# Strassen's form for 14 of 22 gate/up pairs in four feed-forward networks

## The chip, the cores and the metric

One core of a Trainium2 (trn2) chip runs the whole program. The metric is device time in microseconds (us) of one launch, the median of several runs. Engines: PE is TensorE, DVE VectorE, ACT ScalarE, POOL GpSimd; SP issues the loads of weights.

## The reference, cut to what matters

Two blocks follow each other on 512 tokens of width 1024, all in float32. The first has two layers, each with a SwiGLU network, a mixer and another SwiGLU network, and a layer norm after each. The four SwiGLU networks are what the change touches (d_ff 2816):

```python
def swiglu_ffn(x, wi, wo):
    gate, up = jnp.split(x @ wi, 2, axis=-1)
    return (jax.nn.silu(gate) * up) @ wo

def first_block(x, ...):
    alpha = DEEPNORM_ALPHA
    for l in range(DEPTH):
        x = layer_norm(alpha * x + 0.5 * swiglu_ffn(x, ffn1_wi[l], ffn1_wo[l]), ln_g[l, 0], ln_b[l, 0])
        ...
        x = layer_norm(alpha * x + mix, ln_g[l, 1], ln_b[l, 1])
        x = layer_norm(alpha * x + 0.5 * swiglu_ffn(x, ffn2_wi[l], ffn2_wo[l]), ln_g[l, 2], ln_b[l, 2])
    return x
```

The second block (attention branches and a third kind of feed-forward network) is not touched.

## The kernel before, in words

Activations lie transposed: eight tiles of 128 rows (of the width, index k) by 512 tokens. A float32 product is made in three passes of a rounded type: every operand is a high part (the value rounded) and a low part (what is left), and `mm3` (L404) issues weights-high x activations-high, weights-high x activations-low and weights-low x activations-high into one bank of PSUM. The eight tiles of an activation are the objects `X` with lists `h` and `l`.

Weights come in *slabs*, planned ahead in a queue by `plan_w`: a slab is one tile of 128 output columns by 1024 rows, in two raw tiles `wr` of 128x512 (256 KB each). `_dma` (L336) issues the loads on SP up to `raw_bufs` slabs ahead; `_split_hi` (L355) lets ACT copy `wr` into `wh`; `_split_lo` (L364) lets DVE subtract, `wl` = `wr` - `wh`; `slab` (L389) hands out the next slab and splits others ahead, as far as `hl_bufs` allows. The matmuls are thus `m<-xh,wh`, `m<-xl,wh`, `m<-xh,wl`.

One network is `ffn_block1` (L730). It has three parts, `PARTS` (L452): pairs 0 to 5, 6 to 13 and 14 to 21, where pair j is the j-th 128 columns of gate and of up. In each part the pairs are computed (`gemm_tile`, L573, one bank of 512 tokens per slab), then their products go through the down projection (`down`, L678; `out_proj_ln`, L685, in the last part), added to eight tiles `ys`. In part 0 `gemm_first` (L555) does pairs 0 and 1 (four slabs, banks `mf`) as the layer norm's rows come out, and then eight DVE additions make `ys` from the high and low parts. A generator `unit` finishes each pair: silu on ACT (`sg`), product on DVE (`hf`), and the split of it (`hh` on ACT, `hl` on DVE). The last four output tiles run by halves of 256 tokens (banks `mh`), so that the layer norm of the first half begins earlier.

The order of instructions on each engine is written by a scheduler class: `g.s.upto`, `g.s.wait` and `g.s.pump` emit side work (generators that are spawned, here the layer norm's halves) between the matmuls by costs that it holds for each operation. The order stands fixed in the program. All DVE, ACT, POOL and SP instructions are recorded by one helper (L55), all matmuls by another (L279), so rows are told apart by tiles.

Of the kernel before, what the change touches and what calls it, by code (L numbers as in the profile page):

```python
# [223 lines left out]


class G:


    def __init__(self, ctx, tc, raw_bufs=3, hl_bufs=8, f_bufs=90, q_bufs=16):
# [101 lines left out]
    def plan_w(self, w, c0, cols, k0, kt):  # L331

        src = w[k0 * P:(k0 + kt) * P, c0:c0 + cols].rearrange("(k p) c -> p k c", p=P)
        self.plan(lambda t, k, n: self.nc.sync.dma_start(t, src[:, k:k + n]), kt, cols)

    def _dma(self):  # L336
        while self.wi_dma < len(self.wq) and self.wi_dma < self.wi_split + self.raw_bufs:
            load, kt, cols = self.wq[self.wi_dma]
            per = NT // cols
            self.whl_t[self.wi_dma] = parts = []  # L340
            for k0 in range(0, kt, per):
                n = min(per, kt - k0)
                t = self.f("wr", F32, n * cols)
                load(t.rearrange("p (k c) -> p k c", c=cols), k0, n)
                parts.append(t)
            self.wi_dma += 1

    def split_ahead(self, n=1):

        self._dma()  # L350
        while n > 0 and self.wi_split < min(len(self.wq), self.wi_done + self.hl_bufs):
            self._split()
            n -= 1

    def _split_hi(self):  # L355
        parts = []
        for t in self.whl_t[self.wi_hi]:
            hi = self.f("wh", F32R, t.shape[1])
            self.nc.scalar.activation(hi, t, AF.Copy)
            parts.append((t, hi))  # L360
        self.whl_t[self.wi_hi] = parts
        self.wi_hi += 1

    def _split_lo(self):  # L364
        j = self.wi_split
        cols = self.wq[j][2]
        hl = []
        for raw, hi in self.whl_t[j]:
            lo = self.f("wl", F32R, raw.shape[1])
            self.nc.vector.tensor_tensor(lo, raw, hi, ALU.subtract)  # L370
            for k in range(lo.shape[1] // cols):
                c = slice(k * cols, (k + 1) * cols)
                hl.append((hi[:, c], lo[:, c]))
        self.whl_t[j] = hl
        self.wi_split += 1
        self._dma()

    def _split(self):

        if self.wi_hi == self.wi_split:  # L380
            self._split_hi()
        if self.wi_hi == self.wi_split + 1 and self.wi_hi < min(len(self.wq), self.wi_done + self.hl_bufs):
# [68 lines left out]
ALPHA = 4.0 ** 0.25  # L451
PARTS = ((0, 6), (6, 8), (14, 8))  # L452


# [263 lines left out]

def plan_ffn(g, w_a, w_b, hook=None):
    for k0, n in PARTS:  # L720
        for j in range(k0, k0 + n):
            g.plan_w(w_a, j * P, P, 0, KD)
            g.plan_w(w_a, 2816 + j * P, P, 0, KD)
# [6 lines left out]
def ffn_block1(g, xs, gv, bv, hook=None, into=None, by_half=True):  # L730

# [4 lines left out]
    for pi, (k0, n) in enumerate(PARTS):  # L736
        hs = {}

        def unit(j, pg, pu):
# [10 lines left out]
            hs[j] = (hh, hl)  # L750

        j = k0
        if pi == 0:
# [5 lines left out]
            for k in range(KD):  # L759
                nc.vector.tensor_tensor(ys[k], xs.h[k], xs.l[k], ALU.add)  # L760
        while j < k0 + n:
            ps = [gemm_tile(g, xs)]
            pipe.add(unit(j, lambda: ps[0], lambda: ps[1]))
            ps.append(gemm_tile(g, xs))
            pipe.step()
            j += 1
# [1885 lines left out]
def kernel(ctx: ExitStack, tc: tile.TileContext, d, out: bass.AP):  # L2652
# [25 lines left out]
    plan_ffn(g, d["ffn1_wi"][0], d["ffn1_wo"][0])  # L2678
    plan_even(g, d["ev_w_in"][0], d["ev_w_out"][0])
    plan_ffn(g, d["ffn2_wi"][0], d["ffn2_wo"][0])  # L2680
    plan_ffn(g, d["ffn1_wi"][1], d["ffn1_wo"][1])
    plan_odd(g, d["od_w_in"][0], d["od_w_out"][0], lambda l: plan_mem(g, d["w_mem_kv_2"][l]))
    plan_ffn(g, d["ffn2_wi"][1], d["ffn2_wo"][1])
    for l in range(2):
# [25 lines left out]
    with man("f3"):  # L2710
        rx = ffn_block1(g, x, *ln(1, 2),
                            into=lambda: RX(g, [g.f("x") for _ in range(KD)], v["g_pre_mix0"]))
    for l in range(2):
# [41 lines left out]
```

## Time and profile before

| what | value |
|---|---|
| median of 3 runs | 3696.52 us (3695.84 to 3699.57) |
| the profiled execution's own time | 3691.82 us |
| its span (first to last instruction) | 3689.6 us |
| mean granted clock of PE | 0.989 of full speed |
| PE busy | 98% |
| DVE busy | 56% |
| ACT busy | 40% |
| POOL busy | 10% |
| read from memory over the span | 323.65 MB |

The page is one profiled execution. Busy shares are means over the span. The chain is followed back from the last instruction, at each step to what released it. In a timeline a row is one instruction (or a few alike in a row, with their number): its start, its duration, engine, line, operation, tile written and tiles read; in brackets the idle time before it and who ended that. A row's duration on DVE includes a tail in which the next one already runs, so the distance of starts is shorter. In the first part of a network PE runs `mf`, then the `m` of pairs 2 to 5, then `mg` and `m` of the down projection.

### The profile page before, as it was taken

Reading aid. Unit: us, or ns where it says so; the run is one execution under the profiler, and the core shown is the slowest. Engines: PE = TensorE matmul, PEld = TensorE weight load, DVE = VectorE, ACT = ScalarE, POOL = GpSimd, SP = SyncE. Lnnn points to the kernel's source line nnn. Section 1 sums busy time; section 2 is a strip of 40 time slices with the busy share of each in tenths; the row PEclk is TensorE's granted clock in tenths of the full one; section 3 lists DMA queues with packets and bytes.
Section 4 is the critical chain, followed back from the end, with each engine's and each line's share of the span. In section 5 each row is a group of like instructions: output and inputs, shape, how many; then the busy total and the mean of one; then the engine's idle time right before and its main releaser. Section 6 shows DMA issues by size and latency. Waiting matters only on the chain.

```text
span 3689.6 us, 52324 instructions
## 1 busy us (share of the span) xinstructions
PE 3633.5 (98%) x19704; PEld 2982.4 (81%) x19704; DVE 2062.8 (56%) x3771; ACT 1460.8 (40%) x2837; POOL 359.2 (10%) x547
## 2 busy tenths in 40 slices
PE   9999999999999999999999999999999999999999
PEld 7888878888888887677888888788888887888888
DVE  4333878432643266767633375557666745467755
ACT  4223664232333236534422353435333444354433
POOL 0001103000200021010100130022000300130001
PEclk9999999999999999989999999999999999999999
DMA  5333222332333221113233333332333332323231
GB/s 158 100 100 84 75 70 87 104 98 86 89 106 97 86 75 52 39 39 98 84 104 98 90 91 118 89 104 67 99 97 90 105 112 85 100 83 101 86 97 52
DMA packets 615087, 331.78 MB, mean 90 GB/s; under 512 B 25234, under 2 KB 608051, under 8 KB 614835
## 3 DMA queue, kind: packets, MB, share of 16 engines
q1 hardware_dynamic: 612018, 324.81, 30.3%
q10 hardware_dynamic: 2816, 3.64, 0.3%
q8 instruction: 154, 2.52, 0.3%
q14 instruction: 99, 0.80, 0.1%
HBM read 323.65 MB, written 4.74 MB: 89 GB/s over the span
## 4 chain that ended last, share of the span: by engine, by line
PE 91%; DVE 6%; ACT 1%; issue 1%; POOL 0%; DMA 0%; SPq 0%; DVEq 0%; POOLq 0%; ACTq 0%
PE m L279 64%; PE mg L279 5%; PE mf L279 4%; PE mh L279 4%; PE tk L279 3%; PE br L279 2%; DVE wl L55 1%; DVE ln_z L55 1%; DVE x L55 1%; DVE rm_t L55 1%; DVE rst L55 1%; PE st L279 1%; DVE xgl L55 0%; PE S L279 0%; PE mv L279 0%
## 5 line engine op out<-in xcount | busy, mean ns | idle before, releaser
L55 DVE TENSOR_TENSOR wl<-wr,wh 128x512 fp32r<-128x512 f32 (+2 forms) x1208 | 815.3, 720 | 114.9 <-ACT wh L55 114.4
L55 ACT ACTIVATE wh<-wr 128x512 fp32r<-128x512 f32 (+2 forms) x1208 | 663.9, 607 | 93.1 <-PE m L279 50.8
L279 PE MATMUL m<-xh,wh 128*128 128x512 f32 x1544 | 619.6, 401 | 0.0
L279 PE MATMUL m<-xh,wl 128*128 128x512 f32 x1544 | 610.9, 396 | 0.0
L279 PE MATMUL m<-xl,wh 128*128 128x512 f32 x1544 | 610.4, 395 | 0.0
L279 PE MATMUL m<-xgh,wh 128*128 128x512 f32 x1184 | 470.7, 398 | 0.0
L279 PE MATMUL m<-xgl,wh 128*128 128x512 f32 x1184 | 466.3, 394 | 0.0
L279 PE MATMUL m<-xgh,wl 128*128 128x512 f32 x1184 | 466.0, 394 | 0.0
L55 DVE SCALAR_TENSOR_TENSOR hf<-sg,m 128x512 f32<-128x512 f32 x80 | 55.0, 688 | 575.0 <-PE m L279 565.7
L279 PEld LDWEIGHTS m<-xh,wh 128*128 128x128 f32 x1544 | 291.0, 188 | 74.6 <-issue 7.3
L279 PEld LDWEIGHTS m<-xh,wl 128*128 128x128 f32 x1544 | 291.0, 188 | 69.1 <-issue 0.4
L279 PEld LDWEIGHTS m<-xl,wh 128*128 128x128 f32 x1544 | 291.2, 189 | 67.6 <-issue 1.7
L279 PEld LDWEIGHTS m<-xgh,wh 128*128 128x128 f32 x1184 | 222.3, 188 | 55.9 <-issue 5.3
L279 PEld LDWEIGHTS m<-xgh,wl 128*128 128x128 f32 x1184 | 222.3, 188 | 52.4
L279 PEld LDWEIGHTS m<-xgl,wh 128*128 128x128 f32 x1184 | 222.4, 188 | 49.9
L279 PE MATMUL m<-hh,wh 128*128 128x512 f32 x600 | 236.5, 394 | 0.0
L279 PE MATMUL m<-hl,wh 128*128 128x512 f32 x600 | 236.3, 394 | 0.0
L279 PE MATMUL m<-hh,wl 128*128 128x512 f32 x600 | 236.2, 394 | 0.0
L55 ACT ACTIVATE sg<-m 128x512 f32<-128x512 f32 x80 | 47.8, 598 | 424.1 <-PE m L279 424.1
L55 ACT ACTIVATE hh<-hf 128x512 fp32r<-128x512 f32 x88 | 55.7, 633 | 382.6 <-DVE hf L55 382.6
L55 ACT ACTIVATE uc<-up,vecs 128x512 f32<-128x512 f32 x88 | 71.7, 817 | 202.3 <-DVE up L55 202.3
L55 DVE SCALAR_TENSOR_TENSOR uc<-up,vecs,uc 128x512 f32<-128x512 f32 x176 | 131.3, 748 | 12.9 <-ACT uc L55 6.8
(546 smaller groups left out, 6330.3 us busy)
## 6 DMA issues: line engine op xcount, KB each, us to landing
wr<-in_ffn_wi_dram SPq DMA_DIRECT2D x352, 256.0 KB
wr<-in_w_up_dram SPq DMA_DIRECT2D x176, 256.0 KB
wr<-in_ffn_wo_dram SPq DMA_DIRECT2D x160, 256.0 KB
wr<-in_w_in_dram SPq DMA_DIRECT2D x152, 256.0 KB
wr<-in_w_down_dram SPq DMA_DIRECT2D x80, 256.0 KB
wr<-in_od_w_in_dram SPq DMA_DIRECT2D x50, 256.0 KB
wr<-in_ev_w_in_dram SPq DMA_DIRECT2D x48, 256.0 KB
wr<-in_w_out_dram SPq DMA_DIRECT2D x32, 256.0 KB
```

Source lines behind the costliest of these rows:

```text
L55: r = fn(*a, **kw)
L279: return self.nc.tensor.matmul(out, lhsT, rhs, start=start, stop=stop, **kw)
```

## The change

14 of the 22 pairs of each network (`FAST`) are computed in Strassen's form (Winograd's variant). The weights of gate and up of one pair, for the upper and lower 512 rows, are the four blocks A11, A12 (gate) and A21, A22 (up); the activations by halves of the width and of the tokens are the four blocks of B. Seven products of 128x512 by 512x256 take the place of eight:

- `Pair` loads the four blocks as raw tiles and forms four sums of weights on DVE (S1 = A21 + A22, S2 = S1 - A11, S3 = A11 - A21, S4 = A12 - S2).
- `Combos` forms four sums of activations for each of four k, once per network, from `ys` before alpha and the down projection are added, on DVE, and splits them (`th` on ACT, `tl` on DVE).
- `Fast` runs the products in the order A11, S2, A12, S3, S1, A22, S4, each 4 x 3 matmuls of 256 tokens, into four banks, and adds up the banks by `c1` and `c2` on ACT and DVE. `unit_fast` then ends the pair as `unit` does.
- The low part of S2 and of S1 isn't a DVE subtraction: ACT writes the negated high part and POOL issues a DMA that adds the sum to it.
- The slabs of such a pair are single tiles, seven per pair. While `raw_lim` is set, loads are limited to 6 raw tiles and splits to 7 tiles of high parts, and two slabs at most are split per call. This holds from the sums of activations to the last pair; outside it the limits are as before.

```diff
+class Pair:
+    ORDER = ("A11", "S2", "A12", "S3", "S1", "A22", "S4")
+    BY_DMA = ("S2", "S1")
+    FETCH = {"A11": ("A11", "A21"), "S2": ("A22",), "A12": ("A12",)}
...
+    def factor(self, nm):
+        t, TT = self.t, self.g.nc.vector.tensor_tensor
+        if nm == "A11":
+            return t["A11"]
+        if nm == "S2":
+            t["S1"], t["S2"] = self.g.f("ws"), self.g.f("ws")
+            TT(t["S1"], t["A21"], t["A22"], ALU.add)
+            TT(t["S2"], t["S1"], t["A11"], ALU.subtract)
+            return t["S2"]
+        if nm == "S3":
+            TT(t["A21"], t.pop("A11"), t["A21"], ALU.subtract)
+            return t.pop("A21")
+        if nm == "S4":
+            TT(t["A12"], t["A12"], t.pop("S2"), ALU.subtract)
+            return t.pop("A12")
+        return t[nm] if nm == "A12" else t.pop(nm)
...
     def _dma(self):
-        while self.wi_dma < len(self.wq) and self.wi_dma < self.wi_split + self.raw_bufs:
+        while self.wi_dma < len(self.wq) and (
+                self.raw_tiles(self.wi_split, self.wi_dma) < self.raw_lim if self.raw_lim else
+                self.wi_dma < self.wi_split + self.raw_bufs):
...
+    def room(self, i):
+        if i >= len(self.wq):
+            return False
+        if not self.raw_lim:
+            return i < self.wi_done + self.hl_bufs
+        return sum(1 if isinstance(load, Pair) else -(-kt * cols // NT)
+                   for load, kt, cols in self.wq[self.wi_done:i + 1]) <= self.hl_lim
...
-            self.nc.vector.tensor_tensor(lo, raw, hi, ALU.subtract)
+            if isinstance(self.wq[j][0], Pair) and self.wq[j][1] in Pair.BY_DMA:
+                self.nc.scalar.activation(lo, raw, AF.Copy, scale=-1.0)
+                self.nc.gpsimd.dma_start(lo, raw, accum_op=ALU.add)
+            else:
+                self.nc.vector.tensor_tensor(lo, raw, hi, ALU.subtract)
...
+FAST = (4, 5, 6, 7, 9, 10, 12, 13, 14, 15, 17, 18, 20, 21)
+RAW1, HL1 = 6, 7
...
+class Combos:
...
+        for k in range(4):
+            lo, hi = self.ys[k], self.ys[4 + k]
+            s, u = g.f("ta"), g.f("tb")
+            TT(s[:, a], lo[:, b], lo[:, a], ALU.subtract)
+            TT(s[:, b], hi[:, b], s[:, a], ALU.subtract)
+            yield g.pace()
+            TT(u[:, a], hi[:, b], lo[:, b], ALU.subtract)
+            TT(u[:, b], hi[:, a], s[:, b], ALU.subtract)
+            yield g.pace()
+            for nm, t in (("s", s), ("u", u)):
+                h, l = g.f("th", F32R), g.f("tl", F32R)
+                g.split_x(h, l, t)
+                self.t[nm, k] = (h, l)
...
+class Fast:
+    PLACE = {"A11": ("a", 0), "S2": ("a", 1), "A12": ("b", 0), "S3": ("b", 1), "S1": ("d", 1), "A22": ("d", 0),
+             "S4": ("e", 0)}
...
+        w = g.slab()
+        for k in range(4):
+            x = self.cb(nm, k)
+            g.s.upto(*w[k], *x)
+            g.mm3(self.ps[bank][:, HALF[c]], w[k], x, k == 0, k == 3)
...
+        if nm == "S2":
+            c = self.c1 = g.f("c1")
+            nc.scalar.copy(c[:, a], ps("a")[:, a])
+            TT(c[:, b], c[:, a], ps("a")[:, b], ALU.add)
+        elif nm == "S3":
+            u = self.c2 = g.f("c2")
+            c = self.c1
+            TT(u[:, b], c[:, b], ps("b")[:, b], ALU.add)
+            TT(c[:, a], c[:, a], ps("b")[:, a], ALU.add)
...
+        elif nm == "A22":
+            u, c = self.c2, self.c1
+            TT(c[:, b], c[:, b], ps("d")[:, b], ALU.add)
...
+            TT(v(w), v(ps("d")), u[:, None, b].to_broadcast([P, 2, 256]), ALU.add)
...
+        elif nm == "S4":
+            c = self.c1
+            TT(c[:, b], c[:, b], ps("e")[:, a], ALU.add)
...
+            g.raw_lim, g.hl_lim, g.ahead = RAW1, HL1, 2
+            cb = Combos(g, xs, ys)
+            if fast:
+                g.s.spawn(cb.make())
...
+            g.s.wait(lambda: cb.n == 4)
+            if j not in open_:
+                open_[j] = Fast(g, cb)
+            e = open_[j]
+            e.step(nm)
...
+        if pi == len(PARTS) - 1:
+            g.raw_lim, g.ahead = 0, 1
```

How the rows move on two engines, at three places. In the names, a first number is a buffer's or tile's and the rest tells it from others of the program.

**First place: DVE at the start of the third network, from pair 2 to the first fast pair.** Before, `hf` of pair 2 (`hf_1881`) is followed by lo subtractions, two per slab:

```order
L55 SCALAR_TENSOR_TENSOR hf_1881_8865<-sg_1880_8864,m_1888_8879 128x512
L55 TENSOR_TENSOR wl_1891_8908<-wr_1861_8795,wh_1886_8875 128x512
L55 TENSOR_TENSOR wl_1892_8910<-wr_1862_8797,wh_1887_8877 128x512
L55 TENSOR_TENSOR hl_1890_8906<-hf_1881_8865,hh_1889_8905 128x512
L55 TENSOR_TENSOR wl_1900_8949<-wr_1875_8830,wh_1895_8916 128x512
L55 TENSOR_TENSOR wl_1901_8951<-wr_1876_8832,wh_1896_8918 128x512
L55 SCALAR_TENSOR_TENSOR hf_1899_8947<-sg_1898_8946,m_1906_8961 128x512
```

Now, from `hf` of pair 3 (`hf_2253`) on, the sums of activations for k = 2 (at the dots stand six rows of the same pattern for k = 3, and two lo subtractions), and S1 and S2 of the second fast pair (`ws_2290`, `ws_2291`):

```order
L55 TENSOR_TENSOR tl_2264_10951<-tb_2260_10920,th_2263_10950 128x512
L55 SCALAR_TENSOR_TENSOR hf_2253_10906<-sg_2252_10905,m_2258_10918 128x512
L55 TENSOR_TENSOR ta_2267_10961<-y_2164_10439 128x256
L55 TENSOR_TENSOR tb_2268_10962<-y_2168_10443,y_2164_10439 128x256
L55 TENSOR_TENSOR ta_2267_10961<-y_2168_10443,ta_2267_10961 128x256
L55 TENSOR_TENSOR tb_2268_10962<-y_2168_10443,ta_2267_10961 128x256
L55 TENSOR_TENSOR tl_2270_10968<-ta_2267_10961,th_2269_10967 128x512
L55 TENSOR_TENSOR tl_2272_10972<-tb_2268_10962,th_2271_10971 128x512
...
L55 TENSOR_TENSOR wl_2285_11013<-wr_2225_10778,wh_2284_11011 128x512
L55 TENSOR_TENSOR ws_2290_11035<-wr_2226_10780,wr_2234_10819 128x512
L55 TENSOR_TENSOR c1_2288_11031<-c1_2288_11031,m_2279_10989 128x256
L55 TENSOR_TENSOR ws_2291_11036<-ws_2290_11035,wr_2225_10778 128x512
```

The second half of the sums of activations, three lo subtractions and S1 and S2 of pair 5 now stand behind `hf` of pair 3, which reads a bank that PE must end first.

**Second place: PE in the same network, where the first pair that becomes fast begins (before) and in the second fast pair (now).** Before, each matmul is 512 tokens wide, and its low weights come from DVE:

```order
L279 MATMUL m_1915_9002<-xh_1773_8301,wh_1871_8822 128x512
L279 MATMUL m_1915_9002<-xl_1781_8309,wh_1871_8822 128x512
L279 MATMUL m_1915_9002<-xh_1773_8301,wl_1873_8826 128x512
L279 MATMUL m_1915_9002<-xh_1774_8302,wh_1871_8822 128x512
```

Now (bank `m_2308` has the products of A11 and S2, `m_2312` that of A12; `wl_2293` is the low part of S2 that a DMA writes):

```order
L319 MATMUL m_2308_11137<-xh_2128_10256,wl_2285_11013 128x256
L319 MATMUL m_2308_11137<-th_2248_10872,wh_2292_11039 128x256
L319 MATMUL m_2308_11137<-tl_2249_10873,wh_2292_11039 128x256
L319 MATMUL m_2312_11170<-xh_2129_10257,wh_2296_11060 128x256
L319 MATMUL m_2312_11170<-xl_2137_10265,wh_2296_11060 128x256
L319 MATMUL m_2312_11170<-xh_2129_10257,wl_2297_11062 128x256
...
L319 MATMUL m_2312_11170<-xh_2132_10260,wl_2297_11062 128x256
L319 MATMUL m_2308_11137<-th_2248_10872,wl_2293_11041 128x256
```

Twelve matmuls of A12's product stand between the second matmul of S2 and the first that needs its low part. In the other fast pairs that one comes right behind the second.

**Third place: DVE in the layer norm ahead of the third network, at the end of its first half** (`ln_z` and `xl` are the norm's rows). Before:

```order
L55 SCALAR_TENSOR_TENSOR ln_z_1824_8511<-ln_z_1824_8511,vecs_101,rs1_1795_8342 128x256
L55 SCALAR_TENSOR_TENSOR xl_1787_8315<-ln_z_1808_8466,vecs_101,xh_1779_8307 128x256
L55 SCALAR_TENSOR_TENSOR xl_1788_8316<-ln_z_1824_8511,vecs_101,xh_1780_8308 128x256
L55 SCALAR_TENSOR_TENSOR st_v_1826_8544<-st_1825_8541,st_m2_1827_8545 128x256
L55 TENSOR_TENSOR wl_1839_8672<-wr_1750_8151,wh_1837_8668 128x512
```

Now:

```order
L55 TENSOR_TENSOR wl_2172_10447<-wr_2100_10099,wh_2114_10127 128x512
L55 TENSOR_TENSOR wl_2173_10449<-wr_2101_10101,wh_2115_10129 128x512
L55 SCALAR_TENSOR_TENSOR ln_z_2182_10475<-ln_z_2182_10475,vecs_101,rs1_2147_10294 128x256
L55 SCALAR_TENSOR_TENSOR st_v_2184_10484<-st_2183_10481,st_m2_2185_10485 128x256
L55 SCALAR_TENSOR_TENSOR xl_2139_10267<-ln_z_2160_10418,vecs_101,xh_2131_10259 128x256
L55 SCALAR_TENSOR_TENSOR xl_2140_10268<-ln_z_2182_10475,vecs_101,xh_2132_10260 128x256
```

Two lo subtractions of the fourth slab of the coming network, which were made earlier before, stand ahead of the last two `xl`.

## Rows read from the trace of the kernel before

**Rows 1.** The page: busy time by engine, and the chain's shares by engine.

```profile
PE 3633.5 (98%) x19704; PEld 2982.4 (81%) x19704; DVE 2062.8 (56%) x3771; ACT 1460.8 (40%) x2837; POOL 359.2 (10%) x547
...
PE 91%; DVE 6%; ACT 1%; issue 1%; POOL 0%; DMA 0%; SPq 0%; DVEq 0%; POOLq 0%; ACTq 0%
```

**Rows 2.** The chain in order of time, third network: start, us, engine, tile.

```profile
996.40 18.50 PE mf L279 x156
1014.90 44.50 PE m L279 x192
...
1192.97 122.40 PE m L279 x528
```

**Rows 3.** Window of gate/up: length, busy PE, PEld, DVE, ACT, POOL, clock, DMA share, GB/s.

```profile
811.00:944.00 133.00, 133.00 (x575) 107.71 (x574) 44.81 (x72) 35.36 (x64) 0.00 (x0) 1.00 0.33 95
```

**Rows 4.** Timeline of PE: matmuls of 512 columns, and the last output tiles' of 256.

```profile
899.79 0.39 PE L279 MATMUL m<-xh,wl 128*128 128x512 f32 x1
900.02 0.39 PE L279 MATMUL m<-xh,wh 128*128 128x512 f32 x1
...
362.60 0.28 PE L279 MATMUL mh<-hh,wh 128*128 128x256 f32 x1
...
372.52 0.28 PE L279 MATMUL mh<-hh,wh 128*128 128x256 f32 x1
```

**Rows 5.** Timeline of DVE, in a gate/up stretch and in a layer norm.

```profile
900.29 0.69 DVE L55 SCALAR_TENSOR_TENSOR hf<-sg,m 128x512 f32<-128x512 f32 x1 [7.44 <-PE m L279]
900.90 1.29 DVE L55 TENSOR_TENSOR wl<-wr,wh 128x512 fp32r<-128x512 f32 x2
902.10 0.68 DVE L55 TENSOR_TENSOR hl<-hf,hh 128x512 fp32r<-128x512 f32 x1
...
1000.36 0.74 DVE L55 TENSOR_TENSOR ln_z<-y,st 128x256 f32<-128x256 f32 x2
1001.02 0.88 DVE L55 SCALAR_TENSOR_TENSOR ln_z<-ln_z,vecs,rs 128x256 f32<-128x256 f32 x2
```

**Rows 6.** Timeline of ACT in a gate/up stretch.

```profile
894.71 0.60 ACT L55 ACTIVATE sg<-m 128x512 f32<-128x512 f32 x1 [3.16 <-PE m L279]
895.21 1.14 ACT L55 ACTIVATE wh<-wr 128x512 fp32r<-128x512 f32 x2
```

**Rows 7.** Groups by form: count, busy us, mean ns of one, idle before.

```profile
L55 DVE TENSOR_TENSOR wl<-wr,wh 128x512 fp32r<-128x512 f32 x1118 | 776.2, 737 | 114.4 <-ACT wh L55 113.9
...
L55 DVE TENSOR_TENSOR y<-y,mh 128x256 f32<-128x256 f32 x48 | 19.9, 415 | 21.0 <-PE mh L279 21.0
...
L55 ACT COPY y<-mh 128x256 f32<-128x256 f32 x16 | 5.8, 363 | 11.4 <-PE mh L279 11.4
```

**Rows 8.** Timeline of DVE at the start of the third network.

```profile
1011.15 1.29 DVE L55 TENSOR_TENSOR wl<-wr,wh 128x512 fp32r<-128x512 f32 x2
1015.85 0.69 DVE L55 SCALAR_TENSOR_TENSOR hf<-sg,mf 128x512 f32<-128x512 f32 x1 [3.40 <-ACT sg L55]
1017.23 0.69 DVE L55 TENSOR_TENSOR hl<-hf,hh 128x512 fp32r<-128x512 f32 x1 [0.70 <-ACT hh L55]
1017.84 0.68 DVE L55 SCALAR_TENSOR_TENSOR hf<-sg,mf 128x512 f32<-128x512 f32 x1
1018.44 4.90 DVE L55 TENSOR_TENSOR y<-xh,xl 128x512 f32<-128x512 f32 x8
```

**Rows 9.** The chain: loads that it waited for, at the start and alone.

```profile
7.78 5.66 DMA xs<-in_x_dram
...
562.96 2.62 DMA wr<-in_ffn_wi_dram
```

**Rows 10.** Timelines of DVE and POOL at the end of the first network.

```profile
352.24 2.39 DVE L55 TENSOR_TENSOR wl<-wr,wh 128x512 fp32r<-128x512 f32 x2
...
352.46 1.62 POOL L55 TENSOR_TENSOR sum<-y,y 128x512 f32<-128x512 f32 x1 [250.88 <-ACT sq L55]
```

More of the change, by code (lines that the diff above doesn't have):

```diff
@@ L346, in _dma @@
             self.wi_dma += 1
+    def room(self, i):
[5 more added lines that the diff above has]
+                   for load, kt, cols in self.wq[self.wi_done:i + 1]) <= self.hl_lim
     def split_ahead(self, n=1):
         self._dma()
-        while n > 0 and self.wi_split < min(len(self.wq), self.wi_done + self.hl_bufs):
+        while n > 0 and self.room(self.wi_split):
             self._split()
@@ L356, in _split_hi @@
         parts = []
+        load, nm, _ = self.wq[self.wi_hi]
+        if isinstance(load, Pair):
+            self.whl_t[self.wi_hi] = [load.factor(nm)]
         for t in self.whl_t[self.wi_hi]:
@@ L381, in _split @@
             self._split_hi()
-        if self.wi_hi == self.wi_split + 1 and self.wi_hi < min(len(self.wq), self.wi_done + self.hl_bufs):
+        if self.wi_hi == self.wi_split + 1 and self.room(self.wi_hi):
             self._split_lo()
@@ L716, in out_proj_ln, with pair_order, plan_ffn @@
         g.s.spawn(finish(hf))
-def plan_ffn(g, w_a, w_b, hook=None):
-    for k0, n in PARTS:
-        for j in range(k0, k0 + n):
-            g.plan_w(w_a, j * P, P, 0, KD)
-            g.plan_w(w_a, 2816 + j * P, P, 0, KD)
+def pair_order(js, fast):
+    for j in js:
+        for nm in Pair.ORDER if j in fast else (None,):
+            yield j, nm
+def plan_ffn(g, w_a, w_b, hook=None, fast=()):
+    for k0, n in PARTS:
+        pairs = {}
+        for j, nm in pair_order(range(k0, k0 + n), fast):
+            if nm is None:
+                g.plan_w(w_a, j * P, P, 0, KD)
+                g.plan_w(w_a, 2816 + j * P, P, 0, KD)
+            else:
+                if j not in pairs:
+                    pairs[j] = Pair(g, w_a, j * P, 2816 + j * P)
+                g.plan(pairs[j], nm, P)
         for m in range(KD):
@@ L732, in ffn_block1 @@
+def ffn_block1(g, xs, gv, bv, hook=None, into=None, by_half=True, fast=()):
     nc = g.nc
@@ L750, in unit, with unit_fast @@
             hs[j] = (hh, hl)
+        def unit_fast(j, e):
+            sg, hf = e.c1, e.c2
+            nc.scalar.activation(sg, sg, AF.Silu)
+            yield True
+            nc.vector.scalar_tensor_tensor(hf, sg, 0.5, hf, ALU.mult, ALU.mult)
+            hh, hl = g.f("hh", F32R), g.f("hl", F32R)
+            nc.scalar.activation(hh, hf, AF.Copy)
+            yield True
+            nc.vector.tensor_tensor(hl, hf, hh, ALU.subtract)
+            hs[j] = (hh, hl)
         j = k0
@@ L760, in ffn_block1 @@
                 nc.vector.tensor_tensor(ys[k], xs.h[k], xs.l[k], ALU.add)
[L761 to L766, printed above, removed]
+            g.raw_lim, g.hl_lim, g.ahead = RAW1, HL1, 2
+            cb = Combos(g, xs, ys)
+            if fast:
+                g.s.spawn(cb.make())
+        open_ = {}
+        for j, nm in pair_order(range(j, k0 + n), fast):
+            if nm is None:
+                ps = [gemm_tile(g, xs)]
+                pipe.add(unit(j, lambda: ps[0], lambda: ps[1]))
+                ps.append(gemm_tile(g, xs))
+                pipe.step()
+                continue
+            g.s.wait(lambda: cb.n == 4)
[3 more added lines that the diff above has]
+            e.step(nm)
+            if nm == "S4":
+                pipe.add(unit_fast(j, e))
+                del open_[j]
         pipe.drain()
+        if pi == len(PARTS) - 1:
+            g.raw_lim, g.ahead = 0, 1
         of = lambda k, c=slice(0, NT): (hs[k0 + k][0][:, c], hs[k0 + k][1][:, c])
@@ L2711 @@
         rx = ffn_block1(g, x, *ln(1, 2),
-                            into=lambda: RX(g, [g.f("x") for _ in range(KD)], v["g_pre_mix0"]))
+                            into=lambda: RX(g, [g.f("x") for _ in range(KD)], v["g_pre_mix0"]), fast=FAST)
     for l in range(2):
```

81 lines of the change are left out of this document (73 added, 8 removed).

## The prediction

> **What bounds the kernel now.** I read the shares by engine first, then the chain that ended last, then a window inside a feed-forward network (FFN), then single instructions. TensorE (PE) is busy 98% of the span and carries 91% of the chain [rows 1]. The chain in order of time says the same of the FFN that the change touches: matmul group follows matmul group for 100 us and more with nothing between [rows 2]. In the gate/up stretch from 811 to 944 us PE is busy all of it at granted clock 1.00, so at its upper level of 2.4 GHz, while DVE is busy 45 of 133 us, ACT 35, POOL none, and a third of the DMA capacity is in use [rows 3]. So within these FFNs a microsecond of PE removed is a microsecond of time, as long as the other queues, which have room, keep delivering in time.
>
> **Columns removed.** A plain pair (gate and up) is 2 x 8 x 3 = 48 matmuls of 512 columns. A chain row gives 122.40 us for 528 such [rows 2], 0.2318 each, 11.13 us per pair; the timeline shows one starting every 0.23 [rows 4]. A fast pair is 7 products x 4 x 3 = 84 matmuls of 256 columns (the PE rows of the second place above). Matmuls of that width run before in the last output tiles: from 362.60 to 372.52 stand 84 intervals, 9.92 us, 0.118 each [rows 4], with weights changing as in a fast pair. The gain is 11.13 - 9.92 = 1.21 us per pair; 14 pairs in 4 FFNs are 56, so **-67.8 us**. Granted clock stays: PE was never idle before these rows and, if nothing is late, isn't after.
>
> **What DVE gets.** A queued DVE operation costs what it holds the queue: 1.20 for two of 512 columns (900.90 to 902.10), 0.60 each; 0.66 for two of 256 (1000.36 to 1001.02), 0.33 each [rows 5]. A plain pair costs four lo subtractions, hf and hl, 6 x 0.60 = 3.6 of 11.1 us. A fast pair costs five lo, four sums of weights, one 512-column eviction, hf and hl, 12 x 0.60 = 7.2, and five evictions of 256, 1.65: 8.9 us of 9.92. It fits, narrowly. By the means of single operations (737 and 415 ns for lo and eviction [rows 7], 0.69 for hf) it is 12 x 0.73 + 5 x 0.415 = 10.8, over 9.92 for a run of fast pairs, though two fast and one plain (25.2) still stay under PE's 31.0. I take the queued price, since these operations stand back to back; the other is a rival. ACT gets seven hi copies, two negated ones, an eviction, silu and hh: 11 x 0.57 (1.14 for two [rows 6]) + 0.36 [rows 7] = 6.6 us, hidden. Weights read from memory are the same four tiles of 256 KB.
>
> **The new wait: lo of S2 and S1.** POOL queues 112 accumulating DMAs, two per fast pair; PE needs what they write. No such DMA, and none issued by POOL, is in the trace of before. Call L the time from the end of ACT's negated copy to the landing. Nearest rows are loads that the chain waited for: 2.62 us for one of 256 KB, 5.66 where the first eight came together [rows 9]. An accumulating transfer reads the target too, so below 2.62 isn't plausible; a gain is excluded because PE can't use a tile that isn't there. I take the middle, **L = 4.1**, because a third of the DMA capacity is taken beside it [rows 3], and keep both ends.
>
> Second fast pair of a run (seven places per FFN, 28): when the last matmul of S2 of the pair before ends (t), ACT copies its bank (an engine starts 0.27 after the next matmul began: 899.79, 900.02, 900.29 [rows 4, 5]), DVE adds (0.36 and 0.42 [rows 7]), forms S2 of this pair (0.69), ACT writes hi and the negated copy (1.14 [rows 6]); with hand-offs of 0.1 that is t + 3.2. PE needs the lo after six products and two matmuls, 74 x 0.118 = 8.7. So L up to 5.5 costs nothing: **0 us** at 4.1, 28 x 0.16 = 4.5 at 5.66.
>
> Start of each FFN (four): here DVE has sums of activations to make too, and the second fast pair (j = 5) is the tight one. Count from T0, the end of the first matmul group (1014.90 in the third FFN [rows 2]). DVE comes from hf, hl, hf to the y additions at T0 + 3.5 (1018.44) and needs 4.8 for eight [rows 8]. hf of pair 2 starts at T0 + 11.4, hf of pair 3 waits for PE until T0 + 22.25 + 0.27 = 22.5, and the order (first place above) puts it *ahead* of the sums for k = 2 and 3. From there the rows up to S2 of pair 5 are seven lo or tl, S1's sum and hf at 0.60 and nine of 256 columns at 0.33, 8.4 us, and two waits for ACT's copy of a sum (about 0.55 each: a copy of 0.57 and two hand-offs, less one sum beside it; the wait for hh, 0.70, is its like [rows 8]): S2 starts at 32.0, ends at 32.7, ACT's two copies end at 34.0. PE reaches the matmul that needs its lo after the two plain pairs and 110 narrow matmuls (84, and 26 before it in the order of the second place), 22.25 + 13.0 = 35.2. It is late by L - 1.2: 2.9 us at 4.1, 1.4 at 2.62, 4.5 at 5.66. Four starts: **+11.6 us** (5.7 to 18).
>
> **Lookahead at the borders.** Four layer norms now have two more lo subtractions in front of the last xl of the first half (third place): 2 x 0.60 = 1.2 us, if PE waits there for it. 0 to 1.2 each; I take a quarter, since the norm's rows on DVE wait for PE and ACT as well: **+1 us** (0 to 4.8).
>
> **Sum.** -67.8 + 0 + 11.6 + 1 = -55.2. The profiled execution took 3691.8 (span 3689.6 and 2.2 around), so 3636.6; the median of the runs is 4.7 above that execution, so **3641.3 us**. Own range: -67.8 + 5.7 = -62.1, 3634.4, to -67.8 + 4.5 + 18 + 4.8 = -40.5, 3656.0.
>
> **The rivals.**
> 1. *Nothing is late* (L under 1.5, or PE never reaches the wait). Only for: 2.62 is an upper end if part of it is the issue. -67.8: 3628.7. Chance 0.07.
> 2. *POOL and DVE hold each other up.* For: two lo subtractions took 2.39 us instead of 1.29 when a POOL addition began beside them [rows 10, 8], 1.10 more, and DVE will hardly pause in fast stretches. If POOL gets to issue only when the DVE run in progress ends (1.29 to 2.39, taken as 2.0), L = 6.1: 28 x 0.6 + 4 x 4.9 + 1 = 37.4, -30.4: 3666.1. Against: POOL issues here, and does no arithmetic in these stretches [rows 3]. Chance 0.14. The Trainium skill, "SBUF — State Buffer", section "SBUF: two separate sides", has a rule of this kind: GpSimd can't write the descriptors of its own DMAs while VectorE holds the port pair they share, so that a 620 ns DMA took about 3100. An estimate by that page (4.1 + 2.5) is L = 6.6, 28 x 1.1 + 4 x 5.4 + 1 = 53, so 3682; the row of 2.39 agrees with a shared port, but no run here shows a DMA issued by POOL.
> 3. *DVE becomes the bound.* At 10.8 us per fast pair and the 1.10 twice, for its two accumulating DMAs, 13.0: each second pair is 3.1 behind, less the 1.4 of room at L = 4.1: 28 x 1.7 = 47.6, and 4 x (2.9 + 3.1) + 1 = 25: +4.8, no change, 3701. Against: queued operations took 0.60 in every row read. Without the 1.10: 10.8 is 0.9 over, within the room; 4 x 3.8 + 1 = 16, 3645. Chance of the first 0.03.
> 4. *Slower: the accumulating DMA is slow.* Its place is the same 28 + 4, break-even 28 (L - 5.5) + 4 (L - 1.2) + 1 = 67.8, L = 7.05. If reading the target and writing the sum cost a load each in series, 2.62 + 5.66 = 8.28: 28 x 2.78 + 4 x 7.08 + 1 = 107, +39: 3736. For: two rows' worth of latency is possible for a kind of transfer that no row shows. Against: every 256 KB load ran under 5.7 here. Chance 0.06.
>
> That the change doesn't do what it says is no rival: the order has 84 matmuls of 256 columns in each of 56 pairs. The forecast keeps 0.70.
>
> **How the numbers follow.** Two in a thousand of 3700, about 7 us, is what the measurement tells from no change. The range goes from rival 1 (3628) through the forecast to rival 2 (3668): 0.70 + 0.07 + 0.14 = 0.91, less the tails of the forecast. Faster: 0.70 + 0.07 + 0.14 = 0.91; same 0.03; slower 0.06.
>
> **What would show it.** Right: narrow matmuls 0.118 apart for 9.9 us per fast pair; DVE at about nine tenths there; no PE gap in the second pairs of later runs; four gaps of 1.5 to 4.5 us behind the first fast pair of each FFN, at the first matmul with S2's lo, waiting for a POOL DMA; landings about 4 us after the negated copy. Wrong: gaps at many of the 28 places (rivals 2 and 4 by the landing, 3 by DVE with no pause and on-time landings), or narrow matmuls over 0.13 apart, which would take the first term away.

## The result, and the profile after

The median went from 3698.05 to 3645.6 us (four runs each), -52.5 us; the ratio is 0.9856 with an interval of 0.9835 to 0.9877. The prediction said 3641.3 and a range of 3628 to 3668. The profiled execution of the changed kernel took 3646.0 us, with a span of 3644.3. A second round of runs gave 3650.0 against 3695.1, ratio 0.9869 (0.9848 to 0.989).

The page of the changed kernel, the lines that answer to [rows 1], then the new queue and the new transfers (count, size, median us from issue to landing):

```profile
PE 3575.0 (98%) x21720; PEld 3035.3 (83%) x21720; DVE 2414.9 (66%) x4483; ACT 1651.4 (45%) x3206; POOL 452.9 (12%) x659
...
q0 software_dynamic: 16128, 29.37, 5.0%
...
PE 86%; DVE 8%; ACT 2%; issue 2%; DMA 1%; POOL 1%; SPq 0%; DVEq 0%; ACTq 0%; POOLq 0%
...
wl<-ws POOLq DMA_DIRECT2D x112, 256.0 KB, 3.8
```

PE is busy 58 us less, DVE 352 us more, and a new item is on the chain: DMA, with the transfers that make lo of S2 and S1. The chain in order of time through the third network (to be read against [rows 2]) shows where:

```profile
973.63 18.72 PE mf L319 x157
992.35 32.40 PE m L319 x180
...
1026.15 3.90 DMA wl<-ws
1030.09 7.10 PE m L319 x58
1037.19 8.34 PE mg L319 x36
1045.53 106.89 PE m L319 x708
1152.42 11.14 PE mg L319 x48
1163.56 115.18 PE m L319 x744
```

Behind 1037 the network is one run of matmuls again: 708 and 744 without a wait. Ahead of that, one transfer stands on the chain. The window of the second part's gate/up, six fast and two plain pairs (columns as in [rows 3]):

```profile
1070.50:1152.30 81.80, 81.80 (x602) 77.56 (x601) 57.80 (x106) 41.36 (x78) 8.51 (x10) 1.00 0.54 130
```

PE is busy for all 81.8 us; the same eight pairs took 89.0 before. DVE is at 71%, ACT at half.

**One stretch must be taken out of every comparison.** I cut each profile where the chain shows it: each network from the first matmul behind `mf` to the first `mh`, and what lies between. All but one of these stretches agree between two profiles of one kernel to a microsecond. One doesn't: the odd mixer (third network's half tiles to the fourth's `m`) took 455 to 475 us in thirteen profiles, whatever the kernel. Two profiles of the changed kernel, each cut at the same distances from the start of that stretch (columns as in [rows 3], first the change's first profile, then its second):

```profile
1300.86:1473.00 172.14, 171.03 (x1108) 135.29 (x1107) 135.72 (x315) 104.54 (x220) 24.51 (x36) 1.00 0.18 50
1473.00:1533.00 60.00, 57.81 (x863) 40.23 (x862) 41.40 (x86) 30.41 (x47) 0.30 (x3) 0.91 0.16 42
```

```profile
1301.53:1473.67 172.14, 171.03 (x1108) 135.30 (x1107) 135.72 (x315) 104.53 (x220) 24.50 (x36) 1.00 0.18 50
1473.67:1533.67 60.00, 57.80 (x729) 39.80 (x726) 35.10 (x76) 24.17 (x39) 0.30 (x3) 0.76 0.14 37
```

The first 172 us are alike to the instruction. In the next 60 PE is busy 57.8 us in both, but gets through 863 matmuls at a mean granted clock of 0.91 and through 729 at 0.76 (means over its two levels, 1.2 and 2.4 GHz). So the same program in the same order differs by 14.7 us in this one stretch. A spread of 20 us is also what the runs of the kernel before show (3690 to 3710 us), so medians of single rounds are a poor measure here, and the experiments are read by stretches:

| kernel | median us | ratio to before (95%) | networks 1 to 4, sum | first parts, networks 1 to 4 | even mixer | odd mixer |
|---|---|---|---|---|---|---|
| before | 3698.1 | | 1291.9 | 45.5, 44.3, 44.5, 44.6 | 281.6 | 457.3 |
| before, again | 3695.8 | 0.9988 (0.9972 to 1.0003) | 1291.9 | 45.5, 44.3, 44.5, 44.6 | 281.8 | 463.5 |
| change | 3645.6 | 0.9856 (0.9835 to 0.9877) | 1235.6 | 45.2, 44.4, 44.8, 44.9 | 286.4 | 460.6 |
| change, again | 3650.0 | 0.9869 (0.9848 to 0.989) | 1236.5 | 45.2, 44.6, 44.7, 44.8 | 287.2 | 475.3 |
| limits only | 3703.1 | 1.001 (0.9992 to 1.0029) | 1291.4 | 45.4, 44.2, 44.3, 44.5 | 288.2 | 472.8 |
| lo by DVE | 3643.9 | 0.9843 (0.9818 to 0.9867) | 1228.1 | 43.4, 42.1, 42.4, 44.9 | 286.5 | 455.6 |
| pairs 4, 5 plain | 3650.4 | 0.9859 (0.9837 to 0.988) | 1237.4 | 45.5, 44.3, 44.6, 44.5 | 286.5 | 463.7 |
| borders mended | 3642.0 | 0.9833 (0.9807 to 0.9859) | 1235.9 | 45.3, 44.6, 44.5, 44.9 | 281.4 | 455.4 |
| sums early | 3657.5 | 0.9868 (0.9847 to 0.9889) | 1232.1 | 47.3, 42.6, 43.1, 42.7 | 287.1 | 472.4 |
| all three | 3643.1 | 0.9833 (0.9812 to 0.9855) | 1227.4 | 45.6, 41.9, 42.2, 42.1 | 281.7 | 474.4 |
| 18 pairs | 3626.6 | 0.979 (0.9759 to 0.9822) | 1217.6 | 47.2, 42.3, 43.4, 43.2 | 281.5 | 455.4 |
| 18, lo by DVE | 3612.5 | 0.977 (0.9753 to 0.9787) | 1205.7 | 43.4, 41.9, 42.2, 42.1 | 282.0 | 462.6 |
| 18, S1 by DMA | 3613.9 | 0.9778 (0.9752 to 0.9803) | 1209.9 | 45.1, 43.6, 42.6, 42.2 | 279.9 | 457.7 |

"Even mixer" is the stretch from the first network's half tiles to the second's first `m` behind `mf`, layer norms included; a first part ends with the first `mg`.

### The profile page after: what moved, and what is told of

Its sections match the earlier page's. It is cut to its first block, busy times and chain, and to the rows that moved or that the text cites. A ratio compares the mean times of both kernels' runs of the same rounds, so it can differ in the third digit from the quotient of the medians.

```text
span 3644.3 us, 58033 instructions
## 1 busy us (share of the span) xinstructions
PE 3575.0 (98%) x21720; PEld 3035.3 (83%) x21720; DVE 2414.9 (66%) x4483; ACT 1651.4 (45%) x3206; POOL 452.9 (12%) x659
## 4 chain that ended last, share of the span: by engine, by line
PE 86%; DVE 8%; ACT 2%; issue 2%; DMA 1%; POOL 1%; SPq 0%; DVEq 0%; ACTq 0%; POOLq 0%
PE m L319 61%; PE mg L319 5%; PE mf L319 3%; PE tk L319 3%; PE mh L319 3%; PE br L319 2%; DVE wl L55 1%; DVE ln_z L55 1%; DVE rm_t L55 1%; DVE x L55 1%; DMA wl<-ws 1%; DVE xgl L55 1%; DVE rst L55 1%; PE st L319 0%; DVE y L55 0%
## 5 line engine op out<-in xcount | busy, mean ns | idle before, releaser
L55 DVE TENSOR_TENSOR wl<-wr,wh 128x512 fp32r<-128x512 f32 (+2 forms) x1264 | 858.0, 717 | 236.8 <-ACT wh L55 214.9
L319 PE MATMUL m<-xh,wh 128*128 128x512 f32 (+1 forms) x1320 | 456.0, 345 | 0.1
L319 PE MATMUL m<-xh,wl 128*128 128x512 f32 (+1 forms) x1320 | 447.5, 339 | 0.7 <-DVE wl L55 0.7
L319 PE MATMUL m<-xl,wh 128*128 128x512 f32 (+1 forms) x1320 | 446.2, 338 | 0.0
L319 PEld LDWEIGHTS m<-xh,wl 128*128 128x128 f32 x1320 | 249.7, 189 | 30.8 <-DVE wl L55 1.3
L319 PE MATMUL m<-th,wl 128*128 128x256 f32 x896 | 252.2, 282 | 5.8 <-DMA wl<-ws 5.6
L319 PE MATMUL m<-tl,wh 128*128 128x256 f32 x896 | 251.1, 281 | 0.0
L319 PE MATMUL m<-th,wh 128*128 128x256 f32 x896 | 250.0, 281 | 0.0
L55 POOL DMA_DIRECT2D wl<-ws x112 | 96.2, 859 | 1110.1 <-ACT wl L55 782.1
L319 PEld LDWEIGHTS m<-th,wl 128*128 128x128 f32 x896 | 168.7, 188 | 7.7 <-DMA wl<-ws 7.5
```

The costliest lines, as they stand in the source:

```text
L55: r = fn(*a, **kw)
L319: return self.nc.tensor.matmul(out, lhsT, rhs, start=start, stop=stop, **kw)
```

## The experiments

**Is what lies outside the networks scatter?** The kernel before, unchanged.

> The kernel before, unchanged, profiled a second time. Inside the four networks the profiles agree with 56.4 us of gain, outside them the changed one is 11.1 us longer (of which 4.8 in the even mixer, 3.3 in the odd one). If that is scatter between executions, the stretches outside the networks come out 5 to 11 us longer here than in the first profile, and the ratio to before is 1.000. If the change itself costs it, by the lookahead at the borders, they agree with the first profile within 2 us. Either way each network, from the end of its first matmul group to its first half tile, takes 322.6 to 323.8 us.

Measured: the networks again 1291.9 us in sum, the even mixer 281.8, the odd one 463.5 (6.2 more). So 3.3 us in the odd mixer are within its scatter, and the 4.8 of the even mixer are not: that stretch repeats to 0.2 us. Each side was right on one mixer.

**The limits alone.**

```diff
-FAST = (4, 5, 6, 7, 9, 10, 12, 13, 14, 15, 17, 18, 20, 21)
+FAST = ()
```

> The limits of the weight stream as changed, but no pair in Strassen's form. Theory: the limits cost nothing inside the networks (322.6 to 323.8 us each) and at most 1 us at each of the four borders, so within 4 us of before. Rival: the limits are what makes the rest of the program 11 us longer; then this kernel is 8 to 11 us slower than before, with its loss in the even and odd mixers.

Measured: networks 1291.4, so the limits cost nothing inside. The even mixer took 288.2, 6.5 us more than before, and the stretch between the second and third network 49.2 instead of 47.9. My "at most 1 us at each border" fell here: the limits alone lengthen the even mixer. Without the odd mixer (472.8, within its scatter) the span is 9.2 us longer than before, 6.5 of them in the even mixer, so of the rival the size held, and its place for the larger part.

**lo of S2 and S1 by DVE.**

```diff
-    BY_DMA = ("S2", "S1")
+    BY_DMA = ()
```

> The lo parts of S2 and S1 by DVE subtractions instead of accumulating DMAs. Theory: without the 4.1 us to a landing the wait at the start of each network shrinks from 2.3 to 2.8 us to 0.2 to 1, so 6 to 9 us faster than the change; DVE has 8.9 + 1.2 = 10.1 us per fast pair, 0.2 over PE's 9.9, which the plain pair between runs gives back. Rival: DVE, not the DMA, sets the steady pairs; then the second pairs of the 28 runs come late by 0.3 to 2 us each and the kernel is 5 us or more slower than the change.

Measured: networks 7.5 us shorter than the change; the second and third parts keep 81.7 to 82.0. First parts fall to 42.1 and 42.4 us in networks 2 and 3, where the columns alone ask for 96 x 0.2318 + 168 x 0.118 = 42.1. The chain of the third network has no transfer any more:

```profile
987.36 42.40 PE m L319 x264
1029.76 6.02 PE mg L319 x26
```

The fourth network stays at 44.9, with another wait. Its chain, in order of time:

```profile
1778.61 0.64 ACT th L55
1779.25 0.04 issue
1779.30 0.50 PE m L319 x2
```

PE waits there for the split of the last sum of activations, in the first fast pair: the sums for k = 2 and 3 still stand behind hf of pair 3, and here the split of those for k = 1 too, which in the change stands ahead of it. DVE in the fourth network of this run:

```profile
1771.37 0.69 DVE L55 SCALAR_TENSOR_TENSOR hf<-sg,m 128x512 f32<-128x512 f32 x1 [1.61 <-PE m L319]
1773.28 0.69 DVE L55 TENSOR_TENSOR tl<-ta,th 128x512 fp32r<-128x512 f32 x1 [1.22 <-ACT th L55]
```

The DMA was thus one cause of two, and it bought nothing.

**Pairs 4 and 5 plain.**

```diff
-FAST = (4, 5, 6, 7, 9, 10, 12, 13, 14, 15, 17, 18, 20, 21)
+FAST = (6, 7, 9, 10, 12, 13, 14, 15, 17, 18, 20, 21)
```

> Pairs 4 and 5 plain again, so 12 fast pairs per network, and the sums of activations have until pair 6. Theory: the two pairs at the start gain 4 x 2.42 = 9.7 us in columns and the wait for the sums costs 4 x 2.3 to 2.8 = 10, so dropping them changes nothing: within 2 us of the change, first part 44.5 us, second and third parts as they are. Rival: the columns pay in full and the loss lies elsewhere; then it is 8 to 10 us slower than the change.

Measured: networks 1.8 us longer than the change in sum, with two late landings in the second and third parts of networks 3 and 4 (1.0 and 1.1 us). The two pairs at each start gain in columns what the wait takes back, as the theory had it.

**The borders.** In the last part `ahead` stays 2 until the last down projection is through.

```diff
         if pi == len(PARTS) - 1:
-            g.raw_lim, g.ahead = 0, 1
+            g.raw_lim = 0
...
             out_proj_ln(g, ys, of, n, 4, evac, st, finish, head(g, of, n, 2))
+            g.ahead = 1
```

> The change, but two slabs may still be split per call through the last down projection of each network, so that the fourth slab of the next stage is split before the layer norm and not in it; the order of PE outside the networks is then that of the kernel before. Theory: the 4.7 us that the even mixer takes longer after the change come from that order, in which a chunk of the mLSTM (num, den, S) stands ahead of weight matmuls that used to cover its wait. Then the stretch from the first network's half tiles to the second's first matmul group falls from 286.4 to 281.6 to 282.0, the stretch between the second and third from 48.5 to 47.9, the networks stay at 308.2 to 309.4, and the kernel is 4 to 7 us faster than the change. Rival: the mixer is longer because of what the network leaves behind (its loads or its accumulating DMAs); then it stays at 286.

Measured: even mixer 281.4, second to third network 47.8 (change 48.5), tail behind the fourth network 1572.5 (change 1573.6, before 1572.0), networks as they were. The theory holds for the two stretches that it names; the difference behind the fourth network is no larger than what two profiles of the kernel before differ by (1572.0 and 1572.9). In the even mixer PE's order is again that of before. The chain shows what the other order does; first the kernel before, then the change, then this run, at the same place of the even mixer:

```profile
494.98 9.49 PE m L279 x41
504.47 0.86 PE num L279 x2
```

```profile
485.92 1.28 ACT L55
...
487.22 0.59 ACT E L55
...
489.08 0.61 DVE E L55
...
489.73 2.00 PE num L319 x2
491.73 1.68 PE den L319 x2
```

```profile
481.82 8.34 PE m L319 x36
490.16 0.86 PE num L319 x2
```

Before, 41 weight matmuls run while ACT and DVE prepare E (1.28 us of it a table load, then the exponential), and `num` follows at once. After the change `num` stands ahead of them, and PE waits for E. The wait, from the list of PE's waits in the change, and the windows behind it in the change and, later in the mixer, in the kernel before (columns as in [rows 3]):

```profile
PE num L319 <- DVE E L55: 4.0, 1, 4.0
```

```profile
489.70:493.30 3.60, 3.57 (x5) 1.50 (x6) 2.00 (x4) 3.20 (x6) 0.46 (x1) 0.53 0.00 0
```

```profile
573.40:576.90 3.50, 3.17 (x8) 2.54 (x9) 2.07 (x5) 2.22 (x3) 1.06 (x3) 0.52 0.01 2
```

Behind the 4.0 us without a matmul the granted clock is 0.53, close to the lower level of 1.2 GHz, and `num` and `den` take 3.7 us instead of 1.7. The kernel before has such a stretch too, 84 us later (0.52), in which six `mg` and two `num` take 3.6 us; there the change needs 2.1. So 4.0 us of waiting and 2.0 at the lower clock, less 1.5 that the kernel before loses at the lower clock and the change does not, make 4.5 of the 4.8. One slab that is split a little later shifted the order that the scheduler writes 140 us further on.

**The sums of activations earlier.**

```diff
 class Combos:
...
-            yield g.pace()
+            yield g.pace(lead=6000.0)
...
```

The same is done at the other two `yield g.pace()` of the class.

> The change, but the sums of activations may be queued on DVE 6 us ahead and not 2, so that those for k = 2 and half of those for k = 3 stand ahead of hf of pair 3. Theory: hf of pair 3 ahead of the sums is what makes S2 of pair 5 late; with the sums ahead S2 is formed 3 us earlier, its lo lands before PE asks, and the first part falls from 44.4 to 44.9 us (45.2 in the first network) to 42.1 to 42.6 (43.1 to 43.5), the rest as it is: 8 to 10 us faster than the change. Rival: the latency of the accumulating DMA alone sets the wait, wherever the sums stand; then the first parts stay above 44.

Measured: first parts of networks 2 to 4 at 42.6, 43.1 and 42.7, 1.7 to 2.2 us less, a little above what was expected (0.6 to 0.9 of wait for the landing is left). The first network went the other way, to 47.3: PE waits 1.1 us for `th`, 0.6 for `tl` and 1.8 for a landing there. ACT and DVE also set up constants in that network, and a table load of 1.28 us stands on its chain; which of its rows does the harm wasn't taken apart. So the place of the sums behind hf was a cause in three networks, and the rival (latency alone) fell. The DMA's latency is the other cause: lo by DVE takes as much of the wait away in networks 2 and 3 (2.3 and 2.4 us), with the sums left behind hf. For the first network the expectation was wrong.

**All three together.**

```diff
-    BY_DMA = ("S2", "S1")
+    BY_DMA = ()
...
-            yield g.pace()
+            yield g.pace(lead=6000.0)
...
-            g.raw_lim, g.ahead = 0, 1
+            g.raw_lim = 0
...
+            g.ahead = 1
```

> The borders as in the border run, the sums as in the early run, and lo of S2 and S1 by DVE. Theory: the four networks take 305.9 to 307.5 us, the fourth too, where the run with lo by DVE alone waited 2.5 us for the sums of activations; the even mixer's stretch is 281.6 to 282.0; 12 to 16 us faster than the change, so about 3632. Rival: DVE has 10.1 us of work per fast pair of 9.9 and sums in front; then waits of a microsecond come back at the starts and the networks stay over 308.

Measured: networks 2 to 4 at 305.8, 306.1 and 306.1 us, the fourth without its wait, even mixer 281.7. The first network stays at 309.5: the early sums hurt there as in the run before. The profiled execution behind the median of 3643 has an odd mixer of 474 us in it; without that stretch the span is 3168.3 us, against 3183.7 for the change and 3232.3 before.

**18 pairs.** Pairs 4 to 21 all fast, borders and early sums, lo of S2 and S1 by DMA.

```diff
-FAST = (4, 5, 6, 7, 9, 10, 12, 13, 14, 15, 17, 18, 20, 21)
+FAST = tuple(range(4, 22))
```

> Borders and sums as in those runs, lo of S2 and S1 by accumulating DMAs, and pairs 4 to 21 all fast (18 of 22). Theory by queued durations: DVE has 8.9 us per fast pair and keeps up without plain pairs between; gate/up of the second and third part falls from 81.8 to 79.4 us, 19 us in all beside the 14 of the other two edits, so some 30 us faster than the change, if every landing comes within 5.5 us; a landing of up to 6.8 costs 1.3 where it happens. Rival: DVE is the bound at the durations of single operations (10.8 per pair); then the stretches take 8 x 10.8 = 86 us and the kernel is 30 us slower than with 14 pairs.

Measured: gate/up of a part takes 79.6 to 80.6 us. DVE isn't the bound; most of what is over 79.4 are late landings, such as this one of 5.05 us on the chain:

```profile
740.89 5.05 DMA wl<-ws
```

The networks are 18.0 us shorter than the change, and the span without the odd mixer 22.7, not the 30 that were expected: the first network's first part is 47.2 us, as in the run with early sums, and there are the late landings.

**The change, again.**

> The change, unchanged, profiled a second time. The stretches that belong to the change come out as in its first profile: networks 309.4, 308.2, 308.7 and 309.3 us within 0.3, even mixer's stretch 286.4 within 0.3, 48.5 between the second and third. The odd mixer's stretch, which ran 455 to 474 us in the ten profiles so far whatever the kernel, may come out anywhere between. If it is scatter of the chip, the granted clock in its middle goes with its length, and the stretches around it don't move.

Measured: networks within 0.5 us of the first profile, even mixer 0.8 over it, both a little more than I had allowed. In the even mixer the granted clock behind the wait for E differs: 0.56 from 489 to 495 us, against 0.72 in the first profile. The odd mixer took 475.3, with the lower clock shown above.

**18 pairs, lo by DVE.** As the run of 18, with the sums 6 us ahead in networks 2 to 4 alone.

```diff
-    BY_DMA = ("S2", "S1")
+    BY_DMA = ()
...
             cb = Combos(g, xs, ys)
+            cb.lead = 6000.0 if by_half else 2000.0
```

> 18 fast pairs, borders mended, all lo by DVE, sums of activations 6 us ahead except in the first network. Queued durations: 5.4 + 2.4 + 0.6 + 1.65 = 10.1 us of DVE per fast pair, with the down projection's lo on top, against 9.92 of PE: DVE is the bound by 0.2 per pair at least, so gate/up of eight pairs takes 80.8 to 83 us where 79.4 is PE's; first parts 41 to 42 (43.4 in the first network). Rival: DVE catches up in the down projections and the lookahead of seven tiles hides the rest; then 79.4 to 79.8.

Measured: the rival held. Gate/up takes 79.4 to 79.5 us in all eight parts that hold eight pairs, so PE never waits there. The chain of the second network and the window of its second part (columns as in [rows 3]):

```profile
674.21 103.51 PE m L319 x776
```

```profile
698.20:777.60 79.40, 79.40 (x674) 79.40 (x673) 74.48 (x139) 40.11 (x76) 0.00 (x0) 1.00 0.34 100
```

DVE has 14 x 0.60 + 5 x 0.33 = 10.05 us per pair, 80.4 for the 152 operations of eight, but only 139 operations fall into the window, 74.5 us. Others of these pairs are done in the down projections on either side, where DVE has room (15.3 us busy in the 24.0 before the window). By its networks this is the fastest kernel of the study; its median is 3612.5 us, without the odd mixer the span is 35.7 us under that of the change, and no accumulating DMA is in it.

**18 pairs, only S1 by DMA.** As the run before, but

```diff
-    BY_DMA = ()
+    BY_DMA = ("S1",)
```

> As the run before, but lo of S1 by accumulating DMA and only S2, the tight one, by DVE: 9.5 us of DVE per pair of 9.92. S1's lo is needed three products after S2's, 4.2 us later, so a landing of 3.2 to 6.8 us is covered. Theory: no wait is left: gate/up 79.4 to 79.8 in the second and third parts, networks near 301.5, so 12 us under the run of 18 pairs with both by DMA. Rival: S1's landing still ends waits (some 0.3 us at single pairs, as 18 pairs by DMA show); then 80.0 to 80.6.

Measured: in the second and third parts the theory holds (79.4 to 79.5), so S1's landing is covered there. At the starts of networks 1 to 3 waits for a landing are left (1.5, 1.5 and 0.4 us); the networks sum to 1209.9, 4.2 over the run before and 7.7 under 18 pairs with both by DMA, where 12 were expected. So "no wait is left" fell at the starts. PE did not wait for DVE in the run before either, so nothing speaks for the DMA.

## Why the prediction was right, and where not

**Columns: right.** Gate/up of a part fell from 89.03 to 81.78 us in the quietest parts, 7.25 for six pairs, 1.21 each.

**DVE: right in kind.** 6 x 8.9 + 2 x 3.6 = 60.6 us were worked out for such a part; 57.8 are in the window, which holds 106 operations where eight such pairs have 114. The queued price (0.60 and 0.33 [rows 5]) is the one to use: the run of 18 with lo by DVE can't be explained by the means of single operations [rows 7], by which its 139 operations would take some 90 us (14 x 0.73 + 5 x 0.415 = 12.3 per pair, 98 for eight, times 139/152) in a window of 79.4.

**L: right.** The transfers of the changed kernel by their tile (duration of the issue in ns, and us from issue to landing, each least, median, most):

```profile
L55 POOL DMA_DIRECT2D wl<-ws x112: 841/859/1050, 55.4 to 2037.8; - x112
...
DMA to landing us min/median/max: 3.2/3.8/6.8
```

With 0.3 us from ACT's end to the issue that is 4.1. The bounds of 2.62 and 5.66 held the median, not the last few.

**The second pairs: 0 forecast, 1.3 us measured** over 24 places (eight parts, 655.4 in sum against 8 x 81.77). The prediction's 28 counted pair 5 of each network here and again among the starts; at 0 us each this changes nothing in the forecast. Three gaps are of 0.15 us and more, two of them behind landings of 4.7 and 4.8. The room of 5.5 was thus a little too large. The chain of one of the two, in the first network, has S2's sum, the transfer and PE:

```profile
154.09 0.69 DVE ws L55
...
156.25 4.77 DMA wl<-ws
...
161.06 9.00 PE m L319 x72
```

Ahead of that sum DVE has hf of the plain pair, which ends where this run of fast pairs begins, and three lo subtractions. The working had left these out; from the end of ACT's copy, 0.3 before the issue, to PE's need at 160.8 are 4.9 us.

**The starts: 11.6 forecast, 10.0 measured** (2.1, 2.3, 2.8 and 2.8 over what the columns ask, taking for the first network its 45.46 of before less 2.42). The steps came in the order and nearly at the times that the working gave. DVE, ACT, POOL and PE at the start of the third network, T0 being 992.35:

```profile
1014.64 0.69 DVE L55 SCALAR_TENSOR_TENSOR hf<-sg,m 128x512 f32<-128x512 f32 x1 [0.65 <-PE m L319]
1015.25 0.42 DVE L55 TENSOR_TENSOR ta<-y 128x256 f32<-128x256 f32 x1
...
1023.98 0.68 DVE L55 TENSOR_TENSOR ws<-ws,wr 128x512 f32<-128x512 f32 x1
...
1025.24 0.61 ACT L55 ACTIVATE wl<-ws 128x512 fp32r<-128x512 f32 x1
...
1026.15 0.86 POOL L55 DMA_DIRECT2D wl<-ws  x1 [13.67 <-PE m L319]
...
1027.15 0.38 PE L319 MATMUL m<-xh,wl 128*128 128x256 f32 x1 [0.22 <-DVE wl L55]
1030.09 0.38 PE L319 MATMUL m<-th,wl 128*128 128x256 f32 x1 [1.49 <-DMA wl<-ws]
```

hf of pair 3 begins at T0 + 22.3 (forecast 22.5), S2 at 31.6 (32.0), ACT ends at 33.5 (34.0), the lo lands at 37.7. What the working hadn't seen is small: PE loses some of it in two shorter waits before (the second last row), so the wait for the landing itself is 1.5 and not 2.9. In all four starts PE stands idle 5.6 us for landings, in the fourth network for two: S1's low part came late there too (0.5 us), which the working had not counted.

**The borders: the step that failed.** "+1 us (0 to 4.8)" counted two lo subtractions in the layer norms. Measured are 4.8 us in the even mixer, 0.6 between the second and third network and about 1.2 behind the fourth, 6.6 in all, and the larger part isn't in the norms: it is PE's order in the mixer behind, which I had not compared, with a wait of 4.0 us for E and the lower clock behind it. The run with mended borders shows it for the first two, since it gives them back and leaves the networks as they were. The 1.2 behind the fourth is not shown to belong to the change: two profiles of the kernel before differ by 0.9 there, and two runs with mended borders (18 pairs, and 18 with lo by DVE) have 1574 us in that stretch.

Summed with these values the change is -67.8 + 1.3 + 10.0 + 6.6 = -49.9 us. Between the two first profiles it is 45.3, the odd mixer having run 3.3 longer and the first stretch 0.9; the medians say 52.5, and 45.1 in the second round, with the odd mixer's scatter in both. That the forecast of -55.2 lies near the first of them is in part luck of that scatter.

**The rivals.** Nothing late (1) fell by the gaps at the starts, a DVE bound (3) by the two runs of 18 pairs, a slow DMA (4) by the landings. (That "every 256 KB load ran under 5.7" rested on the two loads that the chain shows [rows 9].) POOL and DVE holding each other up (2) fell as well: POOL's issue takes 0.84 to 1.05 us with DVE at 71%. The median landing is 4.2 us in the run of 18 with DVE at 84% (67.39 of 80.00), and 4.0 in the run of 18 with only S1 by DMA, where DVE is at 90% (71.83 of 79.50):

```profile
704.00:784.00 80.00, 79.74 (x673) 79.49 (x672) 67.39 (x127) 47.65 (x90) 12.05 (x14) 1.00 0.63 149
```

```profile
700.00:779.50 79.50, 79.50 (x674) 79.46 (x673) 71.83 (x134) 43.92 (x83) 6.00 (x7) 1.00 0.49 126
```

The rule of the Trainium skill, "SBUF — State Buffer", section "SBUF: two separate sides", by which a DMA issued by GpSimd waits while VectorE holds the port pair that they share, is told there for VectorE's two-port modes, which a float32 tensor copy enters. The prediction's L of 6.6 carried it over to additions and subtractions of two float32 tiles. The traces here show no such wait beside these (L is 4.1, and only the longest landings, of 6.8, come near), which does not contradict the page. What makes these few late stays open. A busier DVE alone is not it: with DVE at 90% the longest landing is 6.3 us, and with 12 fast pairs it is 7.5. The share of the DMA engines goes the same way as the median (0.49, 4.0; 0.63, 4.2), but the change has 3.8 at 0.54, so that isn't shown either.

## What to carry to other kernels

Cost a stage by the engine that it keeps busy, with queued durations, and then walk the first use of what is new: here nearly all of the loss inside the networks (10.0 of 11.3 us) was one chain of four engines at each start, found by counting rows in a queue. Where a scheduler writes the order, compare the order of every stage behind the change, not only of those that it edits: one slab split later cost 4.8 us in a mixer 140 us away. Moving work off an engine that has room, onto a path with a latency, lost here: in each version that was run both ways (14 pairs; 18 pairs, networks 2 to 4) the subtraction on DVE was better than the DMA.

## What the runs showed that was not expected

The granted clock in the middle of the odd mixer differs between executions of one program (0.71 to 0.94 over one eighth of that stretch in the profiles), with the 172 us before it alike in the two profiles of the change, and the stretch takes 455 to 475 us for the same instructions. What sets it isn't shown. PE is busy 96% of the 60 us window there (57.8), with short idle times; in the networks, where it waits only at a few places, the clock was 1.00 in every profile and two profiles agree to half a microsecond. And DVE can be 94% busy for 79 us (74.5 of 79.4) without PE waiting once: the window holds 139 operations where the eight pairs have 152, and the lookahead of seven tiles lets the others run beside the down projections.
